# Two changes to a two-layer encoder kernel: keys and values turned in 32x32 blocks on VectorE, and the early gate and up weights split one part ahead

## The chip, the cores and the metric

The kernel runs on one core of one Trainium2 chip. A core has TensorE (matmuls and their weight loads), VectorE, ScalarE and GpSimd (POOL), and SyncE (SP), which here only issues DMAs; ScalarE and GpSimd issue some DMAs too. Matmul results land in PSUM (eight banks), all else is in SBUF (128 partitions) or in DRAM. The metric is the time of one execution on the device in microseconds; lower is better.

## The reference

What is computed, cut to what matters here (the convolution group, the gates and the norms are left out):

```python
for l in range(DEPTH):                                   # DEPTH = 2, D_MODEL = 1024
    h = h + hybrid_mixer(rmsnorm(h, norm1_w[l]), ...)    # 16 meta tokens + 1024 tokens = 1040 rows
    h = h + swiglu(rmsnorm(h, norm2_w[l]), w_gate_up[l], w_down[l])

# inside the mixer: 4 heads of 128, q and k normalised, v plain
qkv = jax.nn.silu(depthwise_conv_centred(qkv, conv_qkv_w))
o_fwd = chunk_gated_delta_rule(qp, kp, vp, gp[:, :, 0], bp[:, :, 0])
o_bwd = flip(chunk_gated_delta_rule(flip(qp), flip(kp), flip(vp), ...))

# the scan over chunks of tokens
v_new = u_c - w_c @ S
o     = qd_c @ S + a_c @ v_new
S     = S * gl_c + kd_c.T @ v_new

# swiglu
gate, up = jnp.split(h @ w_gate_up, 2, axis=-1)
return (jax.nn.silu(gate) * up) @ w_down
```

The products of the projections are made with each float32 operand split in two parts: a leading one (`hi`, cast on ScalarE) and the rest (`lo`, a subtraction on VectorE). A product is three matmuls: hi x hi, hi x lo, lo x hi.

## The kernel before, in words

**Layout.** Activations lie with channels on the 128 partitions and the 1040 tokens along the free dimension. A projection tile (`inproj`, L313, through `dense`, L144) makes 128 output channels for all tokens: 3 chunks of about 346 tokens (2 of 512 for some tiles of the second layer), each 8 x 3 matmuls into one PSUM bank (L156 to L158). Its weights come as two DMAs of 256 KB on SP (L125) into two `raw` buffers, are split by ScalarE (L126) and VectorE (L127) into three `whi`/`wlo` slots, and an evacuation on VectorE (L319 and others) multiplies by the row norm.

**Order of the work.** The kernel is written once, and a scheduler orders the instructions of each engine by priorities and a simulated time; after that every engine and every DMA queue runs its list in order. The program sets the priorities by hand: evacuations first (`evp`), dense matmuls late (`mmp`), and small jobs in between. Three lists (`jobs`, `jobs2`, `jobs3`) hold closures, and after each chunk of a dense tile one is taken from each list (end of `dense`).

**Stages of a layer.** First the key tiles and the query tiles (`seq`, L675), then four value tiles (L771), then the loop over `(4, 5, 0, 6, 7, 1, 2, 3)` (L805) with four `z` tiles and four convolution tiles (`sc_tile`, L781). Beside them run: `chunk_p` (L486), which makes key-by-key products for nine chunks of tokens (one of 16 meta tokens, eight of 128), `substitute` and `invert`, which invert the triangular matrices (VectorE, then small matmuls), and `chunk_a` (L520), query-by-key products. Then comes the scan (`scan_step`, L839): two directions, nine chunks, its matmuls laid among the dense ones of the convolution tiles and of half of the output projection (`w_out`), its tokens now on partitions. Then the other half of the output projection (`out_part`, L1035), the early gate/up parts, the gate/up tiles, the down projection.

**Turning keys and values.** The scan needs keys and values with tokens on the partitions. Before the change this is done with TensorE. `k_out` (L445), called by `chunk_p`, turns a chunk of keys: four transposes (L451) against an identity into PSUM bank "a", one copy by ScalarE (L453), one store on ScalarE's queue (L454) to `vkd[c, :, 1, :]` in DRAM. `v_store` (L749) does it for a value tile: one transpose of the 16 meta tokens (L753), a copy on VectorE (L757) and a store on SP (L760); and twice four transposes (L764), a copy by ScalarE (L765) and a store on its queue (L766) to `vkd[c, :, 0, :]`. The scan loads both with one row of 512 floats per token (L844, L846 on SP), ordered by head, then by channel. In the scan the keys are the stationary operand of the state update (`su`), the values are an operand of a VectorE addition (L879) and, in the first step, the moving operand.

Tiles of [128, 4, 128] come from one tag, `ck2`, of five buffers (`t2k`).

**The early parts.** While the last output tiles are made, the first products of the gate/up stage that do not need the second half of the tokens are done early: eight parts `(f, q)`, four gate/up rows by two halves of the input channels. `early_part` (L1139) loads 256 KB of weights (L1142), splits them (`w_op`, L1091 on ScalarE and L1092 on VectorE), and makes the product (`prod`, L1109, L1112, L1113), all in one call. Three parts are placed after output tiles 5, 6 and 7 (L1168), five behind the loop (L1199).

Of the kernel before, what the change touches and what calls it, by code (L numbers as in the profile page):

```python
# [17 lines left out]
L = 1040  # L18
H = 4
# [23 lines left out]
def trunk(ctx: ExitStack, tc: tile.TileContext, xT, w_in, w_ba, w_out, w_gu, w_dn,  # L43
# [27 lines left out]
    def pa():  # L71
        return bank("a")
# [229 lines left out]
    for l in range(DEPTH):  # L302
# [142 lines left out]
        def k_out(c, prev):  # L445

            n = 16 if c == 0 else 128
            s0 = 0 if c == 0 else 16 + 128 * (c - 1)
            ps = pa()
            for h in range(H):  # L450
                after(nc.tensor.transpose(ps[0:n, h * 128:(h + 1) * 128], KTt[:, h, s0:s0 + n], ident), prev if h == 0 else None)  # L451
            kt = t2k("kt")
            act(out=kt[0:n].rearrange("p a b -> p (a b)"), in_=ps[0:n], func=AF.Copy)  # L453
            adma(vkd[c, 0:n, 1, :], kt[0:n].rearrange("p a b -> p (a b)"))  # L454


        at0 = [sb.tile([16, 4, 16], F32, tag=f"at0{d}", name=nm("at0")) for d in range(2)]
        P0 = [sb.tile([16, 4, 16], F32, tag=f"P0{d}", name=nm("P0")) for d in range(2)]
# [27 lines left out]
        def chunk_p(c):  # L486
# [1 line left out]
            n, s0 = span(c)  # L488
            kk = bank("b").rearrange("p (h i) -> p h i", h=4)
            for h in range(H):  # L490
                end = mm(kk[0:n, h, 0:n], KTt[:, h, s0:s0 + n], KTt[:, h, s0:s0 + n], start=True, stop=True)
                if h == 0:
                    after(end, last_mm[0])
# [252 lines left out]
            mmp[0] = tc.cur_priority  # L746
            at_prio(here)

        def v_store(i, v, c0):  # L749

            ps = pa()
            if c0 == 0:
                low(lambda: nc.tensor.transpose(ps[0:16, 0:128], v[:, 0:16], ident))  # L753
                vm = t2k("vm")[0:16, 0, :]
                here = tc.cur_priority
                at_prio(evp[0])
                nc.vector.tensor_copy(vm, ps[0:16, 0:128])  # L757
                evp[0] = tc.cur_priority
                at_prio(here)
                dma(vkd[0, 0:16, 0, i * 128:(i + 1) * 128], vm)  # L760
            else:
                vt = v[:, 16 + 128 * (c0 - 1):16 + 128 * (c0 + 3)]
                for c in range(4):
                    low(lambda: nc.tensor.transpose(ps[:, c * 128:(c + 1) * 128], vt[:, 128 * c:128 * c + 128], ident))  # L764
                act(out=vt, in_=ps, func=AF.Copy)  # L765
                adma(vkd[c0:c0 + 4, :, 0, i * 128:(i + 1) * 128].rearrange("c p e -> p c e"), vt.rearrange("p (c e) -> p c e", c=4))  # L766

        ca = [0, 1, 8, 2, 7, 3, 6, 4, 5]
        st1 = sub_start(1)
        jobs3.extend([None, None, None, st1[0], st1[1], None, st1[2], st1[3], st1[4]])  # L770
        for i in range(4):  # L771
            t = trow()
            if i == 3:
                jobs3.extend([None] * 3 + invert(0))
            inproj(8 + i, to_row(t))
            v = trow() if i % 2 == 0 else row(Y[1] + "f")
            conv(t, v, P_CV + 3 * (8 + i))
            act(out=v, in_=v, func=AF.Silu)
# [60 lines left out]
        def scan_step(d, c, first, final, tied=False):  # L839
            n = 16 if c == 0 else 128  # L840
            s0 = 0 if c == 0 else 16 + 128 * (c - 1)
            base = d * 2048
            V, K, A, sz = (rec[:, base + 512 * i:base + 512 * i + 512].rearrange("p (h e) -> p h e", h=4) for i in range(4))
            dma(V[0:n].rearrange("p h e -> p (h e)"), vkd[c, 0:n, 0, :])  # L844
            if not final:
                dma(K[0:n].rearrange("p h e -> p (h e)"), vkd[c, 0:n, 1, :])  # L846
# [289 lines left out]
        early, bks0 = {}, {}  # L1136
        turn_e = [None]

        def early_part(f, q):  # L1139
# [22 lines left out]
        for m in range(KT + 2):  # L1162
# [514 lines left out]
```

## Time and profile before

| what | value |
|---|---|
| time, median of 3 runs | 2462.8 us |
| lowest and highest run | 2461.87 and 2466.39 us |
| the profiled execution, its own time | 2463.0 us |
| span of its instructions | 2461.2 us |
| TensorE busy | 2441.9 us (99%) |
| VectorE busy | 1782.3 us (72%) |
| ScalarE busy | 1056.0 us (43%) |
| DMA | 335.26 MB, mean 136 GB/s |

How to read it: times are in microseconds from the start of the span unless marked ns. PE is TensorE's matmul, PEld its weight load, DVE is VectorE, ACT ScalarE, SP SyncE; a "q" behind a name means that engine's sequencer or queue. L156 is line 156 of the kernel. A name such as `pacc<-a,whi` says which tile is written from which. A matmul's length in a row includes the time in the pipeline, so neighbours overlap; busy time counts a moment once. A row of busy times by stretch has the stretch, its length, then busy time and count for TensorE, its weight loads, VectorE, ScalarE and GpSimd, then the granted TensorE clock, the DMA share and GB/s.

### The profile page before, as it was taken

Reading aid. Unit: us, or ns where it says so; the run is one execution under the profiler, and the core shown is the slowest. Engines: PE = TensorE matmul, PEld = TensorE weight load, DVE = VectorE, ACT = ScalarE, POOL = GpSimd, SP = SyncE. Lnnn points to the kernel's source line nnn. Section 1 sums busy time; section 2 is a strip of 40 time slices with the busy share of each in tenths; the row PEclk is TensorE's granted clock in tenths of the full one; section 3 lists DMA queues with packets and bytes.
Section 4 is the critical chain, followed back from the end, with each engine's and each line's share of the span. In section 5 each row is a group of like instructions: output and inputs, shape, how many; then the busy total and the mean of one; then the engine's idle time right before and its main releaser. Section 6 shows DMA issues by size and latency. Waiting matters only on the chain. (4 is left out here: it accounts for less than half of the span.)

```text
span 2461.2 us, 44853 instructions
## 1 busy us (share of the span) xinstructions
PE 2441.9 (99%) x17530; PEld 2255.1 (92%) x17530; DVE 1782.3 (72%) x3296; ACT 1056.0 (43%) x1964; POOL 67.0 (3%) x157
## 2 busy tenths in 40 slices
PE   9999999999999999999999999999999999999998
PEld 8999999999999999999999988999978888888887
DVE  6888346769877777877657984457697777678774
ACT  6654434535333333444446543335453333234444
POOL 0120000000000000000000200000000000000002
PEclk9999999999999999999999999999999999999999
DMA  4445344534223332674224452445332233237641
GB/s 134 162 156 184 118 134 158 181 102 144 97 95 104 111 104 78 210 239 148 89 87 148 159 178 105 159 142 197 123 124 99 94 116 112 91 107 257 203 131 69
DMA packets 201320, 335.26 MB, mean 136 GB/s; under 512 B 23404, under 2 KB 88356, under 8 KB 201108
## 3 DMA queue, kind: packets, MB, share of 16 engines
q1 hardware_dynamic: 172996, 293.83, 36.0%
q10 hardware_dynamic: 25936, 34.19, 4.3%
q0 software_dynamic: 2176, 4.36, 0.6%
q8 instruction: 138, 2.26, 0.4%
q14 instruction: 74, 0.61, 0.1%
HBM read 250.31 MB, written 81.99 MB: 135 GB/s over the span
## 5 line engine op out<-in xcount | busy, mean ns | idle before, releaser
L156 PE MATMUL pacc<-a,whi 128*128 128x346 f32 (+1 forms) x800 | 260.2, 326 | 0.2 <-ACT a L176 0.2
L158 PE MATMUL pacc<-a,wlo 128*128 128x346 f32 (+1 forms) x800 | 259.0, 325 | 0.1
L156 PE MATMUL pacc<-b,whi 128*128 128x346 f32 (+2 forms) x672 | 232.4, 347 | 0.0
L158 PE MATMUL pacc<-b,wlo 128*128 128x346 f32 (+2 forms) x672 | 231.6, 346 | 0.3 <-DVE wlo L127 0.2
L157 PE MATMUL pacc<-a,whi 128*128 128x346 f32 (+1 forms) x681 | 221.9, 326 | 0.6 <-DVE a L177 0.6
L126 ACT ACTIVATE whi<-raw 128x512 fp32r<-128x512 f32 x166 | 104.6, 632 | 240.5 <-PE pacc L157 194.3
L157 PE MATMUL pacc<-b,whi 128*128 128x346 f32 (+2 forms) x580 | 200.1, 345 | 0.0
L156 PEld LDWEIGHTS pacc<-a,whi 128*128 128x128 f32 x800 | 150.5, 188 | 2.4 <-issue 1.0
L127 DVE TENSOR_TENSOR wlo<-raw,whi 128x512 fp32r<-128x512 f32 x166 | 114.2, 689 | 52.7 <-ACT whi L126 52.0
L158 PEld LDWEIGHTS pacc<-a,wlo 128*128 128x128 f32 x800 | 150.7, 189 | 1.4 <-issue 0.8
L158 PEld LDWEIGHTS pacc<-b,wlo 128*128 128x128 f32 x672 | 126.4, 188 | 10.5 <-issue 1.7
L156 PEld LDWEIGHTS pacc<-b,whi 128*128 128x128 f32 x672 | 126.4, 188 | 9.7 <-issue 0.8
L157 PEld LDWEIGHTS pacc<-a,whi 128*128 128x128 f32 x681 | 128.3, 188 | 4.7 <-issue 2.1
L1091 ACT ACTIVATE whi<-rw 128x512 fp32r<-128x512 f32 x92 | 57.9, 633 | 138.1 <-PE pf L1112 37.3
L157 PEld LDWEIGHTS pacc<-b,whi 128*128 128x128 f32 x580 | 109.2, 188 | 7.9 <-issue 1.0
L1091 ACT ACTIVATE b<-rw 128x512 fp32r<-128x512 f32 x64 | 40.2, 632 | 136.3 <-PE pacc L1112 38.9
L1091 ACT ACTIVATE a<-rw 128x512 fp32r<-128x512 f32 x64 | 40.2, 631 | 103.2 <-PE pacc L1112 62.6
L319 DVE TENSOR_TENSOR b<-pacc,rstd 128x346 f32<-128x346 f32 (+1 forms) x63 | 32.3, 513 | 48.8 <-PE pacc L158 48.7
L1092 DVE TENSOR_TENSOR wlo<-rw,whi 128x512 fp32r<-128x512 f32 x92 | 62.9, 686 | 2.9 <-ACT whi L1091 2.1
L319 DVE TENSOR_TENSOR a<-pacc,rstd 128x346 f32<-128x346 f32 (+2 forms) x59 | 32.7, 554 | 42.4 <-PE pacc L158 42.3
L1113 PE MATMUL pacc<-b,wlo 128*128 128x260 f32 (+1 forms) x172 | 52.7, 306 | 0.0
L1112 PE MATMUL pacc<-b,whi 128*128 128x260 f32 (+1 forms) x172 | 52.7, 306 | 0.0
(965 smaller groups left out, 7846.9 us busy)
## 6 DMA issues: line engine op xcount, KB each, us to landing
raw<-in_w_in SPq DMA_DIRECT2D x110, 256.0 KB
raw<-in_w_gu SPq DMA_DIRECT2D x104, 256.0 KB
rw<-in_w_gu SPq DMA_DIRECT2D x88, 256.0 KB
rw<-in_w_dn SPq DMA_DIRECT2D x94, 192.0 KB
rec<-vkd SPq DMA_DIRECT2D x61, 256.0 KB
raw<-in_w_out SPq DMA_DIRECT2D x48, 256.0 KB
b<-ad SPq DMA_DIRECT2D x45, 260.0 KB
a<-ad SPq DMA_DIRECT2D x45, 256.0 KB
```

What stands on the lines that cost most here:

```text
L126: whi_done[0] = act(out=hi, in_=raw[:, 0:kk, :], func=AF.Copy)
L127: whi_done[1] = tt(out=lo, in0=raw[:, 0:kk, :], in1=hi.bitcast(F32), op=ALU.subtract)
L156: mm(ps[:, :n], wh, xh[:, n0:n1], start=(i == 0), stop=False)
L157: mm(ps[:, :n], wh, xl[:, n0:n1], start=False, stop=False)
L158: last_mm[0] = mm(ps[:, :n], wl, xh[:, n0:n1], start=False, stop=(i == K - 1))
L319: tt(out=t[:, n0:n1], in0=ps, in1=rstd[:, n0:n1], op=ALU.mult)
L1091: act(out=hi, in_=src, func=AF.Copy)
L1092: tt(out=lo, in0=src, in1=hi.bitcast(F32), op=ALU.subtract)
L1112: mm(ps[:, :CW], w[0][:, k, :], tl[:, cs], start=False, stop=False, skip_group_check=True)
L1113: one = mm(ps[:, :CW], w[1][:, k, :], th[:, cs], start=False, stop=stop and k == nk - 1, skip_group_check=True)
```

## The change

`turned(c, w, src)` replaces the transposes on TensorE. VectorE transposes each 32x32 block of a [128, 4 heads, 128 tokens] tile, and writes it so that channel and head are interleaved, head fastest. A block transpose leaves a token's channels in four groups of 32 partitions, so four DMAs, one for each 32 channels, put them in place in `vkd`: runs of 128 floats (512 bytes). Two of the four of a key chunk go on ScalarE's queue, all others on SP. Values are first stored to DRAM as they are (`vd`, one store per tile on SP) and loaded back chunk by chunk for all four heads (`kv_load`), one job ahead of their transpose (`v_turn`). The nine keys and values are turned in ten jobs, put in the list when the fourth tile of the loop (the third `z` tile) begins; before, keys were turned in `chunk_p` and values right behind their tiles. In DRAM a token's row is now ordered by channel, then by head, so the scan's key and value operands have a step of four floats.

The early weights get a call of their own, `early_weights`, placed one part ahead of the product that uses them (two ahead in the last parts). The order of the parts is the same.

```diff
+        vd = dram.tile([4, 128, L], F32, name=nm("vd"))
+
+        def turned(c, w, src):
 
             n = 16 if c == 0 else 128
-            s0 = 0 if c == 0 else 16 + 128 * (c - 1)
-            ps = pa()
-            for h in range(H):
-                after(nc.tensor.transpose(ps[0:n, h * 128:(h + 1) * 128], KTt[:, h, s0:s0 + n], ident), prev if h == 0 else None)
-            kt = t2k("kt")
-            act(out=kt[0:n].rearrange("p a b -> p (a b)"), in_=ps[0:n], func=AF.Copy)
-            adma(vkd[c, 0:n, 1, :], kt[0:n].rearrange("p a b -> p (a b)"))
-
+            m = max(n, 32)
+            t = t2k("tn").rearrange("p a b -> p (a b)")[:, 0:4 * m].rearrange("p (j b h) -> p j b h", h=4, b=32)
+            nc.vector.transpose(out=t.rearrange("p j b h -> p h j b"), in_=src.rearrange("p h (j b) -> p h j b", b=32))
+            for i in range(4):
+                if c == 0:
+                    (adma if w and i > 1 else dma)(vkd[0, 0:16, w, 128 * i:128 * i + 128], t[32 * i:32 * i + 16, 0].rearrange("p b h -> p (b h)"))
+                else:
+                    (adma if w and i > 1 else dma)(vkd[c].rearrange("(j a) w e -> a j w e", a=32)[:, :, w, 128 * i:128 * i + 128], t[32 * i:32 * i + 32].rearrange("p j b h -> p j (b h)"))
+
+        def kv_load(c):
+
+            n, s0 = span(c)
+            m = max(n, 32)
+            t = t2k("vm")[:, :, 0:m]
+            dma(t, vd[:, :, s0:s0 + m].rearrange("h p t -> p h t"))
+            turned(c, 1, KTt[:, :, s0:s0 + m])
+            vload[c] = t
+
+        def v_turn(c):
+            turned(c, 0, vload.pop(c))
+
+        vload = {}
...
-            k_out(c, end)
...
-            jobs.extend([lambda i=i, v=v, c0=c0: v_store(i, v, c0) for c0 in (0, 1, 5)])
+            dma(vd[i], v)
...
             if j == 3:
                 jobs3.extend(invert(1))
+                jobs.extend([lambda i=i: (kv_load(ca[i]) if i < 9 else None, v_turn(ca[i - 1]) if i else None) for i in range(10)])
...
-            V, K, A, sz = (rec[:, base + 512 * i:base + 512 * i + 512].rearrange("p (h e) -> p h e", h=4) for i in range(4))
-            dma(V[0:n].rearrange("p h e -> p (h e)"), vkd[c, 0:n, 0, :])
+            V, K, A, sz = (rec[:, base + 512 * i:base + 512 * i + 512] for i in range(4))
+            dma(V[0:n], vkd[c, 0:n, 0, :])
             if not final:
-                dma(K[0:n].rearrange("p h e -> p (h e)"), vkd[c, 0:n, 1, :])
+                dma(K[0:n], vkd[c, 0:n, 1, :])
+            V, K = (t.rearrange("p (e h) -> p h e", h=4) for t in (V, K))
...
+        EARLY = [(0, 0), (1, 0), (0, 1), (1, 1), (2, 0), (3, 0), (2, 1), (3, 1)]
+        ew = {}
+
+        def early_weights(i):
+            f, q = EARLY[i]
             A = raw4("raw")
             dma(A, w_gu[l, f, 0, :, 4 * q:4 * q + 4, :])
-            w = w_op(A, True)
+            ew[f, q] = w_op(A, True)
+
+        def early_part(f, q):
+
+            w = ew.pop((f, q))
...
-            for f, q in {5: [(0, 0)], 6: [(1, 0)], 7: [(0, 1)]}.get(m, ()):
-                early_part(f, q)
+            if 5 <= m < 8:
+                early_part(*EARLY[m - 5])
+            if 4 <= m < 8:
+                early_weights(m - 4)
+            if m == 8:
+                early_weights(4)
...
-        for f, q in ((1, 1), (2, 0), (3, 0), (2, 1), (3, 1)):
-            early_part(f, q)
+        for i in range(3, 8):
+            early_part(*EARLY[i])
+            if 5 <= i + 2 < 8:
+                early_weights(i + 2)
```

The lines of `v_store` that go are told above.

More of the change, by code (lines that the diff above doesn't have):

```diff
@@ L443, in normalise @@
                 tt(out=dst[:, h, :], in0=dst[:, h, :], in1=bc, op=ALU.mult)
-        def k_out(c, prev):
+        vd = dram.tile([4, 128, L], F32, name=nm("vd"))
+        def turned(c, w, src):
             n = 16 if c == 0 else 128
-            s0 = 0 if c == 0 else 16 + 128 * (c - 1)
-            ps = pa()
-            for h in range(H):
-                after(nc.tensor.transpose(ps[0:n, h * 128:(h + 1) * 128], KTt[:, h, s0:s0 + n], ident), prev if h == 0 else None)
-            kt = t2k("kt")
-            act(out=kt[0:n].rearrange("p a b -> p (a b)"), in_=ps[0:n], func=AF.Copy)
-            adma(vkd[c, 0:n, 1, :], kt[0:n].rearrange("p a b -> p (a b)"))
+            m = max(n, 32)
[16 more added lines that the diff above has]
+        vload = {}
         at0 = [sb.tile([16, 4, 16], F32, tag=f"at0{d}", name=nm("at0")) for d in range(2)]
@@ L490, in chunk_p @@
             for h in range(H):
-                end = mm(kk[0:n, h, 0:n], KTt[:, h, s0:s0 + n], KTt[:, h, s0:s0 + n], start=True, stop=True)
+                one = mm(kk[0:n, h, 0:n], KTt[:, h, s0:s0 + n], KTt[:, h, s0:s0 + n], start=True, stop=True)
                 if h == 0:
-                    after(end, last_mm[0])
-            k_out(c, end)
+                    after(one, last_mm[0])
             for d in (dirs0 if c == 0 else (0, 1)):
@@ L747, in low @@
             at_prio(here)
[L749 to L766, printed above, removed]
         ca = [0, 1, 8, 2, 7, 3, 6, 4, 5]
@@ L842, in scan_step @@
             base = d * 2048
-            V, K, A, sz = (rec[:, base + 512 * i:base + 512 * i + 512].rearrange("p (h e) -> p h e", h=4) for i in range(4))
-            dma(V[0:n].rearrange("p h e -> p (h e)"), vkd[c, 0:n, 0, :])
+            V, K, A, sz = (rec[:, base + 512 * i:base + 512 * i + 512] for i in range(4))
+            dma(V[0:n], vkd[c, 0:n, 0, :])
             if not final:
-                dma(K[0:n].rearrange("p h e -> p (h e)"), vkd[c, 0:n, 1, :])
+                dma(K[0:n], vkd[c, 0:n, 1, :])
+            V, K = (t.rearrange("p (e h) -> p h e", h=4) for t in (V, K))
+            A, sz = (t.rearrange("p (h e) -> p h e", h=4) for t in (A, sz))
             if c > 0:
@@ L1137, in trunk @@
         turn_e = [None]
-        def early_part(f, q):
+        EARLY = [(0, 0), (1, 0), (0, 1), (1, 1), (2, 0), (3, 0), (2, 1), (3, 1)]
+        ew = {}
+        def early_weights(i):
+            f, q = EARLY[i]
             A = raw4("raw")
             dma(A, w_gu[l, f, 0, :, 4 * q:4 * q + 4, :])
-            w = w_op(A, True)
+            ew[f, q] = w_op(A, True)
+        def early_part(f, q):
+            w = ew.pop((f, q))
             if q == 0:
```

## The prediction

> **What bounds the kernel now.** I read the page first, then what TensorE waits for, then the busy time by stage.
>
> ```profile
> span 2461.2 us, 44853 instructions
> PE 2441.9 (99%) x17530; PEld 2255.1 (92%) x17530; DVE 1782.3 (72%) x3296; ACT 1056.0 (43%) x1964; POOL 67.0 (3%) x157
> PEclk9999999999999999999999999999999999999999
> ```
>
> TensorE is busy from end to end at the full granted clock, so what counts is what is taken from TensorE's own queue, and which waits it keeps. Its waits by releaser (total us, times, longest):
>
> ```profile
> PE pb L1113 <- DVE wlo L1092: 1.7, 2, 1.4
> PE pa L753 <- ACT b L765: 1.2, 1, 1.2
> ...
> PE pf L1113 <- DVE wlo L1092: 0.8, 1, 0.8
> ...
> PE pa L1113 <- DVE wlo L1092: 0.7, 1, 0.7
> ...
> PE pacc L158 <- DVE wlo L127: 0.2, 1, 0.2
> ```
>
> Two of these causes are touched: one value transpose that waited for its PSUM bank, and the early gate/up products (L1113) that waited for VectorE's half of the weight split. The stages, with TensorE, weight-load, VectorE and ScalarE busy time and counts:
>
> ```profile
> 150.00:215.00 65.00, 63.77 (x720) 60.56 (x719) 59.42 (x136) 34.20 (x46) 6.34 (x12) 1.00 0.38 120
> 260.00:310.00 50.00, 50.00 (x699) 47.62 (x698) 12.48 (x25) 19.14 (x35) 0.00 (x0) 1.00 0.34 116
> 563.00:605.00 42.00, 40.42 (x334) 39.23 (x333) 41.26 (x65) 26.45 (x48) 0.00 (x0) 1.00 0.39 126
> 1385.00:1455.00 70.00, 69.87 (x710) 62.06 (x709) 64.07 (x143) 34.91 (x46) 6.34 (x12) 1.00 0.43 137
> 1490.00:1550.00 60.00, 60.00 (x711) 52.52 (x710) 16.87 (x30) 20.90 (x38) 0.00 (x0) 1.00 0.34 117
> 1785.00:1830.00 45.00, 42.01 (x216) 33.31 (x215) 43.13 (x66) 26.49 (x42) 0.00 (x0) 1.00 0.41 135
> ```
>
> The rows are, for layers 0 and 1, the value rows (150, 1385), the stage to which the turning moves (260, 1490) and the early gate/up parts (563, 1785). VectorE is nearly full in the first kind, idle three quarters of the time in the second, and full in the third.
>
> **Part 1, what is removed.** A matmul's row shows its latency; what it costs is the distance to the next start. A block of four value transposes, then a single one (16 meta tokens), in the timeline of TensorE (start, length):
>
> ```profile
> 161.65 0.32 PE L158 MATMUL pacc<-a,wlo 128*128 128x346 f32 x1
> 161.81 0.60 PE L764 MATMUL pa<-ident,b 128*128 128x128 f32 x4
> 162.16 0.40 PE L156 MATMUL pacc<-a,whi 128*128 128x346 f32 x1
> 162.40 0.32 PE L157 MATMUL pacc<-a,whi 128*128 128x346 f32 x1
> ```
> ```profile
> 156.12 0.32 PE L157 MATMUL pacc<-a,whi 128*128 128x348 f32 x1
> 156.28 0.27 PE L753 MATMUL pa<-ident,b 128*16 128x128 f32 x1
> 156.31 0.41 PE L158 MATMUL pacc<-a,wlo 128*128 128x348 f32 x1
> 156.55 0.32 PE L156 MATMUL pacc<-a,whi 128*128 128x348 f32 x1
> ```
>
> From 161.65 to 162.40 are 0.75 us, in which two dense matmuls take 0.16 each (161.65 to 161.81 shows one): the block costs 0.75 - 0.32 = 0.43. The single one costs 0.43 - 0.32 = 0.11. Counts, from the whole span for L451 (keys), L764 and L753 (values); the two numbers after the stretch are busy time and count on TensorE, then on its weight loads:
>
> ```profile
> 0.00:2461.00 2461.00, 10.80 (x72) 8.41 (x72) 1.00 0.41 136
> 0.00:2461.00 2461.00, 9.76 (x64) 7.69 (x64) 1.00 0.41 136
> 0.00:2461.00 2461.00, 2.18 (x8) 0.70 (x8) 1.00 0.41 136
> ```
>
> 72 + 64 are 34 blocks: 34 x 0.43 = 14.6 us. Eight singles: 0.9 us. The bank wait of L753 goes too, since nothing else takes bank "a" there: 1.2 us. Together **-16.7 us**, all in TensorE's own queue. ScalarE's 34 copies out of PSUM and VectorE's eight go as well; they were beside TensorE's work, so I count nothing.
>
> **Part 1, what is added.** Per layer 18 block transposes on VectorE (16 of 512 columns, 2 of 128). The kernel has the same instruction on 1024 columns:
>
> ```profile
> L571 DVE STREAM_TRANSPOSE b<-x x1: 2192/2192/2192, 242.3 to 242.3; 128x1024 f32<-128x1024 f32 x1
> L571 DVE STREAM_TRANSPOSE a<-x x1: 2054/2054/2054, 1475.2 to 1475.2; 128x1024 f32<-128x1024 f32 x1
> ```
>
> About 1.05 us for half of it, so 16 x 1.05 + 2 x 0.3 = 17 us per layer. They lie in the stages that begin at 260 and 1490, where VectorE has 37.5 of 50 and 43.1 of 60 us free: hidden. Were the cover gone they would cost 34 us in all.
>
> DMAs: SP gains four stores of V rows, nine loads of turned-to-be values and 54 of the 72 quarter stores per layer, and loses four small stores; ScalarE gets the other 18 quarter stores and loses 17 stores. Issue costs:
>
> ```profile
> L846 SPq DMA_DIRECT2D rec<-vkd x31: 319/320/425, 295.8 to 1675.7; - x31
> L766 ACTq DMA_DIRECT2D vkd<-b x4: 366/369/378, 164.6 to 204.6; - x4
> ```
>
> POOL's queue is not passed. 63 x 0.37 = 23 us per layer on SP, which has no other work than to issue; on ScalarE one issue of 0.37 more, against 17 copies less. New waits: a value transpose waits on VectorE for its load, and behind it stand PSUM evictions (L319) and weight splits (L127); a quarter store waits on SP and on ScalarE for the transpose, and behind it stand the weight loads (L125), the scan's loads, and ScalarE's splits (L126). TensorE waits for the splits. Bounds: nothing (the value load is issued one job ahead of its transpose) up to rival B's sum. The nearest row, the wait for L127 above, is 0.2 us in the whole kernel; I take **+1 us**.
>
> The scan takes its loads from what the turning stores. It starts at 295 and 1534, and has slack: the last transposes of its output, and the first product that needs all of it:
>
> ```profile
> 499.90 0.60 PE L958 MATMUL pa<-ident,b3f 128*128 128x128 f32 x4
> ...
> 527.12 0.28 PE L156 MATMUL pf<-o,whi 128*128 128x260 f32 x1
> ...
> 1731.84 0.60 PE L958 MATMUL pa<-ident,a3f 128*128 128x128 f32 x4
> ...
> 1749.07 0.28 PE L156 MATMUL pf<-o,whi 128*128 128x256 f32 x1
> ```
>
> 27 and 17 us of dense matmuls follow it, so a scan that starts up to 17 us late costs nothing.
>
> The scan now reads keys and values with a step of four floats: 31 key tiles (the count of L846), four weight loads each, 124 in all, and the value operand of the VectorE additions. No row shows TensorE reading at such a step. Low end: nothing, and not below, as no work goes away. High end: the scan's matmuls start 0.112 us apart, eight of them in 0.90 us:
>
> ```profile
> 447.07 1.06 PE L861 MATMUL pb<-vv,P 128*128 128x128 f32 x8
> 447.97 1.06 PE L861 MATMUL pf<-vv,P 128*128 128x128 f32 x8
> ```
>
> A weight load twice as long adds 0.112 each: 124 x 0.112 = +13.9 us. The nearest row is VectorE's own: the transposes above, read or written at a step, take 2.0 to 2.1 ns a column, a plain operation less:
>
> ```profile
> L127 DVE TENSOR_TENSOR wlo<-raw,whi 128x512 fp32r<-128x512 f32 x166 | 114.2, 689 | 52.7 <-ACT whi L126 52.0
> ```
>
> That is 1.35 ns a column, a ratio of 1.5, but transposing itself may be the reason. On TensorE the load runs beside the matmul before it (92% and 99% busy on the page), so I take nothing and keep 13.9 as rival A. [...] On VectorE a slower value read would add some 0.13 us (128 columns at 1 ns) to each of four additions a step, 5 us in nine steps: inside the 17.
>
> **Part 2.** The early weights are loaded and split one part before they are used. At most the three L1113 rows go: 1.7 + 0.8 + 0.7 = 3.2 us. But VectorE is full in those stages (41.26 of 42, 43.13 of 45), the splits are only reordered, and TensorE then meets the next operand that VectorE owes. I take **-2 us** of 0 to -3.2.
>
> **Sum.** -16.7 + 1 - 2 = -17.7 us. The profiled execution took 2463.0 us (span 2461.2), 0.2 above the median of 2462.8; on the median that is **2445 us**.
>
> **The rivals.**
>
> A, strided keys: the reads above cost 13.9 us on TensorE, which has nothing to hide them: 2459. For it: the step is new, and the scan's TensorE work is dense. Against: the pairs are pipelined.
>
> B, slower than before: SP issues in order, and a quarter store that waits for a late value load holds the weight load behind it. Waits of SP between 260 and 310, and the longest landing in the chain that ended last:
>
> ```profile
> SPq L125 <- DVE wlo L127: 33.4, 5, 13.7
> ```
> ```profile
> 1819.71 6.11 DMA raw<-in_w_gu
> ```
>
> A load of 6.1, a transpose of 1.05 and four issues of 0.37 hold SP for 8.6 us. A weight slot comes free about one chunk (24 matmuls at 0.16 = 3.8 us) ahead of need, so TensorE would wait 4.8 us for each load caught. Five loads wait there per layer; from four caught in all (19 us) the gain is gone; at five to a layer, half of it overlapped with other waits, the sum is +24: 2469. For it: 63 more entries in that queue. Against: those five loads wait up to 13.7 us for their slot anyway, so the queue has time between them.
>
> C, VectorE becomes the bound in the crowded stages: the value rows' stage would shrink below its 59.4 and 64.1 us of VectorE work (I count 2 us lost per layer), and part 2 gives nothing back (2 us): 2451. For it: the busy rows above. Against: the last substitution steps on VectorE aren't needed until the next stage.
>
> **How the numbers follow.** Forecast 0.50, A 0.20, B 0.13, C 0.17. The bound for "same" is 0.2%, 4.9 us, about what a measurement of this kernel can tell from no change: 2457.9 to 2467.7. Faster: the forecast, C, and 0.07 of A (a partial penalty), 0.74. Same: 0.13 of A and 0.02 of B, 0.15. Slower: the rest of B, 0.11. The range reaches from all early stalls gone and some hidden transitions more (2438) to just past A (2461); outside lie B and a few hundredths of the others.
>
> **What would show it.** Right: no L451, L764 or L753 rows on TensorE, some 144 matmuls fewer, its busy time down by about 16 us; the 0.112 us spacing kept where the keys are weights; VectorE's new transposes near 1.05 us, in the stages with room; no new TensorE wait over 1 us. A: key products spaced 0.2 us. B: new TensorE waits for the splits between 260 and 310, behind SP waits for quarter stores. C: L1113 or L1109 waits as long as before. The forecast is wrong if the scan's end passes the first product that needs it, or if the key spacing grows.

## The result, and the profile after

| | before | after |
|---|---|---|
| time, median (lowest to highest) | 2463.9 us (2461.9 to 2466.4) | 2504.9 us (2502.4 to 2506.3) |
| ratio to before, 95% interval | 1 | 1.0165 [1.0147, 1.0182] |
| profiled execution, its span | 2463.0, 2461.2 us | 2506.3, 2504.3 us |

The forecast was 2445 us, and the range ended at 2461: wrong by 60 us, and in sign. The head of the page of after, span and busy time:

```profile
span 2504.3 us, 44778 instructions
PE 2475.6 (99%) x17386; PEld 2286.4 (91%) x17386; DVE 1823.3 (73%) x3324; ACT 1036.8 (41%) x1930; POOL 66.2 (3%) x157
```

TensorE has 144 matmuls fewer, and still it is busy 34 us longer. Two places show where. The first is the scan. The same group of matmuls at the same place of the work, in TensorE's timeline (start, length, count), before and then after:

```profile
452.63 1.05 PE L861 MATMUL pb<-vv,rec 128*128 128x128 f32 x8
453.51 0.61 PE L861 MATMUL pf<-vv,rec 128*128 128x128 f32 x4
453.96 1.06 PE L861 MATMUL pb<-vv,rec 128*128 128x128 f32 x8
454.85 1.50 PE L861 MATMUL pf<-vv,rec 128*128 128x128 f32 x12
456.11 0.40 PE L157 MATMUL pacc<-a,whi 128*128 128x346 f32 x1
```
```profile
470.53 1.05 PE L860 MATMUL pb<-vv,rec 128*128 128x128 f32 x8
471.42 1.09 PE L860 MATMUL pf<-vv,rec 128*128 128x128 f32 x4
472.35 2.03 PE L860 MATMUL pb<-vv,rec 128*128 128x128 f32 x8
474.21 1.99 PE L860 MATMUL pf<-vv,rec 128*128 128x128 f32 x12
475.96 0.40 PE L157 MATMUL pacc<-a,whi 128*128 128x346 f32 x1
```

Before, the 32 matmuls (16 float32 products of two each) take 3.48 us to the next dense matmul, after 5.43. Eight with attention tiles as weights (these lie in `rec` too) still take 0.89 us to the next start; the eight with keys as weights take 1.86 (472.35 to 474.21), 0.23 apart in place of 0.11. The weight loads (min/median/max ns) fit that:

```profile
L860 PEld LDWEIGHTS pf<-vv,rec x256: 186/256/332, 312.6 to 1775.2; 128*128 128x128 f32 x120, 16*128 16x128 f32 x8
L860 PEld LDWEIGHTS pb<-vv,rec x248: 187/193/332, 309.6 to 1748.5; 128*128 128x128 f32 x124
```

Together these are 504 loads for 252 products: 124 have keys as weights, 128 attention tiles. Before, all took 181 to 193 ns. Now 248, two for each product with keys, take more than 300, 330 in the median, and the other 256 at most 209.

The second place is the stage of the turning. A window of 60 us from 250 (PE busy and count, PEld, DVE, ACT, POOL, granted clock, DMA share, GB/s), before and then after:

```profile
250.00:310.00 60.00, 60.00 (x762) 57.62 (x761) 19.14 (x34) 22.73 (x40) 0.00 (x0) 1.00 0.36 123
```
```profile
250.00:310.00 60.00, 57.75 (x701) 54.14 (x700) 30.28 (x41) 20.71 (x37) 0.00 (x0) 0.91 0.70 199
```

TensorE gets through 61 matmuls fewer, waits 2.25 us and has 0.91 of its clock. The window after holds the same stage, though not quite the same instructions. VectorE has 30 us free in it, yet what counts is its order. VectorE's timeline, with the wait ahead of an instruction in brackets, and TensorE's:

```profile
269.37 1.06 DVE L452 STREAM_TRANSPOSE tn<-b 128x512 f32<-128x512 f32 x1
274.33 1.08 DVE L452 STREAM_TRANSPOSE tn<-vm 128x512 f32<-128x512 f32 x1 [3.90 <-DMA vkd<-tn]
275.26 0.67 DVE L127 TENSOR_TENSOR wlo<-raw,whi 128x512 fp32r<-128x512 f32 x1
```
```profile
273.41 0.33 PE L157 MATMUL pacc<-a,whi 128*128 128x348 f32 x1
275.98 0.43 PE L158 MATMUL pacc<-a,wlo 128*128 128x348 f32 x1 [2.25 <-DVE wlo L127]
```

A transpose needs one of the five `ck2` buffers, and waits 3.90 us until the quarter stores of an earlier chunk have landed and freed one. Behind it stands a weight split, and TensorE waits for that split. Then the clock drops. Six windows of after at half clock (the third column from the right):

```profile
277.20:284.00 6.80, 6.80 (x45) 6.31 (x44) 4.62 (x6) 3.78 (x7) 0.00 (x0) 0.50 0.93 259
304.50:307.90 3.40, 3.40 (x13) 3.40 (x13) 0.00 (x0) 1.10 (x4) 0.00 (x0) 0.51 0.86 255
314.80:318.20 3.40, 3.40 (x12) 3.40 (x13) 1.48 (x5) 0.00 (x0) 0.00 (x0) 0.50 0.58 211
1465.10:1471.90 6.80, 5.48 (x65) 5.41 (x65) 4.00 (x10) 1.76 (x3) 0.00 (x0) 0.50 0.48 170
1567.50:1574.30 6.80, 6.80 (x26) 6.03 (x24) 1.21 (x2) 2.27 (x7) 0.00 (x0) 0.50 0.70 239
1581.10:1584.50 3.40, 3.40 (x14) 3.40 (x13) 0.64 (x2) 0.00 (x0) 0.00 (x0) 0.50 0.32 111
```

30.6 us at half clock are about 15.3 us of work lost (an estimate from the clock of 0.50 in these rows; the account below has 15.7); before has such a window only at its very end. (After has a seventh, of 3.4 us at 55, ahead of all changed work; e4_early_only below, which turns on TensorE as before does, has it too.) TensorE's longest waits in after follow. The three of 2 us and more begin at 273.7, 1463.7 and 1562.4, close to the three long windows; the second window begins while its wait lasts.

```profile
PE pacc L158 <- DVE wlo L127: 3.7, 4, 2.2
PE pf L614 <- issue: 2.7, 1, 2.7
PE pb L860 <- DMA rec<-vkd: 2.0, 1, 2.0
```

**The account.** I gave each matmul the usual distance to the next start of its shape (lower quartile in before) and summed: that is TensorE's work. What the starts really took beyond it is the rest: slow loads, half clock and waits.

| kernel | span | matmuls | work | rest | of it waits and gaps over 1 us |
|---|---|---|---|---|---|
| before | 2461.2 | 17530 | 2350.6 | 102.5 | 5.2 |
| after | 2504.3 | 17386 | 2335.0 | 161.3 | 16.9 |
| e1_step_only | 2501.3 | 17530 | 2350.6 | 142.6 | 5.5 |
| e2_blocks | 2456.2 | 17386 | 2335.0 | 113.6 | 14.0 |
| e5_own_place | 2451.5 | 17386 | 2335.0 | 108.8 | 9.2 |
| e8_two_rings | 2453.2 | 17386 | 2335.0 | 110.6 | 13.5 |
| e9_in_place | 2457.4 | 17386 | 2335.0 | 114.8 | 13.4 |
| e13_two_behind | 2460.2 | 17386 | 2335.0 | 117.4 | 15.9 |

So 15.6 us of work went, and 58.8 us of rest came. Sorted by what a start met, of the 58.8 are 34.5 in scan matmuls with an operand from `rec` at full clock, 15.7 at half clock, 10.7 in waits of over 0.25 us, and -2.1 in everything else. The account is of one profiled execution for each kernel: that of e2_blocks was the fastest of its ten (5.2 us under their median), that of e8_two_rings also lies 5.2 under its median, that of e5_own_place 1.6 over it.

### The profile page after: what moved, and what is told of

Read it like the earlier page. It is cut to its first block, busy times and chain, and to the rows that moved or that the text cites. A ratio compares the mean times of both kernels' runs of the same rounds, so it can differ in the third digit from the quotient of the medians.

```text
span 2504.3 us, 44778 instructions
## 1 busy us (share of the span) xinstructions
PE 2475.6 (99%) x17386; PEld 2286.4 (91%) x17386; DVE 1823.3 (73%) x3324; ACT 1036.8 (41%) x1930; POOL 66.2 (3%) x157
## 5 line engine op out<-in xcount | busy, mean ns | idle before, releaser
L127 DVE TENSOR_TENSOR wlo<-raw,whi 128x512 fp32r<-128x512 f32 x166 | 113.9, 687 | 45.9 <-ACT whi L126 45.4
L1090 ACT ACTIVATE whi<-rw 128x512 fp32r<-128x512 f32 x92 | 57.8, 633 | 132.7 <-PE pf L1111 36.9
L1090 ACT ACTIVATE b<-rw 128x512 fp32r<-128x512 f32 x64 | 40.1, 630 | 141.1 <-PE pacc L1111 38.5
L1090 ACT ACTIVATE a<-rw 128x512 fp32r<-128x512 f32 x64 | 40.2, 630 | 103.7 <-PE pacc L1111 60.7
```

The lines of the kernel that those rows point to most:

```text
L127: whi_done[1] = tt(out=lo, in0=raw[:, 0:kk, :], in1=hi.bitcast(F32), op=ALU.subtract)
L1090: act(out=hi, in_=src, func=AF.Copy)
```

## The experiments

Theory S: the read at a step of four floats makes the loss. Rival theories: VectorE's or SP's queue in the turning stage, or part 2.

**e1_step_only**, before with the scan's views alone:

```diff
-V, K, A, sz = (rec[...].rearrange("p (h e) -> p h e", h=4) for i in range(4))
+V, K = (t.rearrange("p (e h) -> p h e", h=4) for t in (V, K))
+A, sz = (t.rearrange("p (h e) -> p h e", h=4) for t in (A, sz))
```

> The kernel before, in which only the scan's view of its key and value tiles is changed to a step of four floats; everything else, the TensorE transposes and the plain storage included, stays, so the channels and heads of keys and values reach the scan exchanged. Theory 1 (the step on TensorE): in the changed kernel the scan's pairs of weight load and matmul whose weights are keys stand 0.23 us apart instead of 0.112, and there are 248 of them, since each of the 124 float32 products is two pairs; so 248 x 0.12 = +30 us here: 2494 us, all of it in the scan. Theory 2 (waits): the changed kernel's loss comes from VectorE waiting for stores of turned tiles, the TensorE waits behind it and the half clock that follows; then this kernel, which has none of these, stays within 5 us of 2464.

Measured: 2503.5 us, ratio 1.0157 [1.0142, 1.0172]. The step alone costs 39 us, 9 more than theory 1 has; after is 41 us slower, with 15.6 us less work. The rest of e1 is 40.1 above before's, with 266 starts 0.215 to 0.26 us apart in the scan, where before has none. Its waits of over 1 us are before's (5.5 us against 5.2), and still it has two windows of 3.4 us at half clock in the scan (at 315 and 1574), where after has its windows at 314.8 and 1581.1.

**e2_blocks**, after with rows by block, head and channel, so that VectorE turns without a step on its output and the scan reads runs of 32 floats (the keys by four loads in place of one):

```diff
-t = ...rearrange("p (j b h) -> p j b h", h=4, b=32)
+t = ...rearrange("p (j h b) -> p j h b", h=4, b=32)
-dma(K[0:n], vkd[c, 0:n, 1, :])
+for i in range(4):
+    dma(K[0:n].rearrange("p (h i b) -> p i h b", h=4, i=4)[:, i], vkd[c, 0:n, 1, :].rearrange("p (i h b) -> p i h b", h=4, i=4)[:, i])
```

> The changed kernel with a token's row stored in blocks of 32 channels, head by head (block, head, channel) instead of channel by channel, so nothing has a step of four floats: the block transposes write runs of 32, keys are put in plain order by four loads of 128-byte runs in place of one, values are read in four runs of 32. Theory 1: the 248 key pairs go back to 0.112 us, -30 us, and the three half-clock windows inside the scan (10 us at half clock, 5 us) with them: 2470 to 2475 us. Theory 2: the waits stay as they are, 2500 to 2510 us. More DMA issues on SP (three more per key load, 93 in all) can cost a few us under both.

Measured: 2463.1 us, 0.9992 [0.9982, 1.0001], 7 us under the range of theory 1. All of the loss is gone, and of the 15.6 us of shorter work next to nothing is kept: 11.1 came back as rest in the profiled execution, and 14.3 by the medians (15.6 less the 1.3 us that it is faster than before). The transposes are faster too, by shape in after and then in e2_blocks:

```profile
L452 DVE STREAM_TRANSPOSE tn<-vm x18: 395/1089/1152, 253.3 to 1555.9; 128x512 f32<-128x512 f32 x16, 128x128 f32<-128x128 f32 x2
```
```profile
L452 DVE STREAM_TRANSPOSE tn<-vm x18: 302/711/715, 254.9 to 1528.8; 128x512 f32<-128x512 f32 x16, 128x128 f32<-128x128 f32 x2
```

Their length was not the price: VectorE still waits for buffers, 29.8 us against 26.4 in after (total, times, longest), and TensorE's wait for a split is still there:

```profile
DVE tn L452 <- DMA vkd<-tn: 29.8, 10, 7.3
```
```profile
PE pacc L158 <- DVE wlo L127: 2.7, 2, 2.4
PE pb L639 <- ACT P L646: 2.5, 1, 2.5
```

The second row, a wait in layer 1 at 1525, goes through ScalarE. Two of the four stores of a key chunk are on its queue; it issues four at 1519.39, 1519.89, 1522.71 and 1526.14, and the copies that TensorE needs come behind the last (the profile puts the end of that wait down to a value load):

```profile
1519.39 7.06 ACTq L457 DMA_DIRECT2D vkd<-tn  x4
1526.50 0.59 ACT L644 ACTIVATE a<-pb 64x512 f32<-64x512 f32 x1 [7.54 <-DMA vm<-vd]
```

**e3_turn_only** and **e4_early_only**: after without part 2, and before with part 2 alone.

```diff
 e3: -w = ew.pop((f, q))
 e3: +A = raw4("raw")
 e3: +dma(A, w_gu[l, f, 0, :, 4 * q:4 * q + 4, :])
 e3: +w = w_op(A, True)
 e4: the part-2 lines of the diff above, on before
```

> The changed kernel with the early parts as before (weights loaded and split in the same call as their product). If part 2 gives what was forecast, this is 2 us slower than the changed kernel: 2507. If the splits are only reordered and another operand is late instead, it is the same within 3 us: 2502 to 2508. If part 2 does harm, it is faster by 3 us or more.

> The kernel before with part 2 alone: 2462 us if the L1113 waits go as forecast (-2 of at most -3.2), 2464 if other operands are late in their place. Neither theory on the keys touches it.

Measured: e3 2503.9 us, 1.0155 [1.0138, 1.0171], and after 1.0165; e4 2464.6 us, 1.0000 [0.9991, 1.0010]. Part 2 is worth nothing that can be measured. TensorE's waits of after from 555 to 660 say why:

```profile
PE pacc L1108 <- DVE a L998: 1.3, 1, 1.3
PE pa L1112 <- DVE wlo L1091: 0.6, 1, 0.6
```

The splits come earlier, and the wait goes to the activations (L998) that the same VectorE owes; in layer 1 it goes to ScalarE's half of a split (L1090, 1.3 us).

Then the step itself, on before: **e6_values_step** has only the values at a step of four, **e7_keys_two** only the keys at a step of two.

```diff
 e6: +V = V.rearrange("p (e h) -> p h e", h=4)
 e7: +K = K.rearrange("p h e -> p (h e)").rearrange("p (g e k) -> p g k e", g=2, k=2)
```

> The kernel before with one change: only the values of a scan step are read at a step of four floats (channels and heads are exchanged in the values, so the output is another); the keys are read as before. e1_step_only, with both at the step, cost 39 us. Theory L (it is the weight load of the keys, 248 pairs at 0.23 us in place of 0.112): this costs only the first step's value products and at most 3 us of half clock, 2465 to 2470 us, and the scan's weight loads stay at 192 ns. Rival V (the values are read by VectorE between the first and the second group of products, 124 operations at 431 ns where before has 343, which would be 10.9 us if each stood on the path): 2475 us.

> The kernel before with one change: the keys of a scan step are read at a step of two floats, 8 bytes (heads and channels are exchanged in pairs, so the output is another); the values are read as before. It asks whether the price of the step is a threshold or grows with it. If the price grows with the bytes passed, a third of that at a step of four: a key pair spaced 0.15 us, 248 times 0.039, 2474 us. [...] If any step costs in full: 248 times 0.118 and half clock, 2495 us.

Measured: e6 2470.3 us, 1.0028 [1.0016, 1.0040]; e7 2465.5 us, 1.0005 [0.9995, 1.0014]. A step of two floats costs nothing that can be measured: neither 2474 nor 2495 us came, and the loads from `rec` take at most 201 ns. Four cost in full (up to 332 ns a load in e1_step_only), so the price does not grow evenly with the step; three was not tried, and why two are free and four are not is not shown. In e6 VectorE's operation with the values takes 430 ns in place of 343, 124 times (0.09 us each, 11 us in all), and the time leaves no room for that. What costs there is the first step, where the values are the moving operand (eight matmuls in 1.62 us to the next start, 0.80 in before):

```profile
303.18 1.98 PE L863 MATMUL pb<-rec,P 128*128 128x128 f32 x8
304.80 0.52 PE L158 MATMUL pacc<-a,wlo 128*128 128x346 f32 x1
```

30 starts in the scan are 0.215 to 0.26 us apart, 3.6 us, and two windows of 3.4 us at half clock follow (at 308 and 1550), 3.4 us. Measured are 5.6 us by the medians; the profiled execution, from which these sums are, was 2.6 over its median. So of e1's 39 us about 33 are the keys, by subtraction.

That left the turning. Theory W: VectorE stands in its order until a store has landed and freed a buffer, and what TensorE needs stands behind it. **e5_own_place** gives every turned tile but chunk 0's a place of its own:

```diff
-t = t2k("tn")...
+t = (KTt, QT)[w][:, :, s0:s0 + 128].rearrange("p j (h b) -> p j h b", b=32)
```

> The kernel with rows by block, head and channel (e2_blocks), and one change: except for chunk 0, the turned keys go into the chunk's slots of the query array and the turned values into its slots of the key array, which nobody reads any more at that point, in place of the ring of five 2-KB buffers. So a block transpose no longer waits until an earlier quarter store has landed and given a buffer back; operations, stores and loads are the same in number and size. In e2_blocks TensorE issues 15.6 us less work than before (2335.0 against 2350.6 us, each matmul at its usual spacing) but loses 11.1 us more in excess spacing (113.6 against 102.5), 8.8 of it in waits of over 1 us. Theory W (VectorE waits in order for buffers, the weight splits queued behind it come late, TensorE stops for over 2 us and then runs for some 3.4 to 7 us at half clock): the row of 29.8 us on turned buffers falls below 3 us, the wait of 2.4 us for a low weight part goes, and the time is 2449 to 2454 us. Rival S (the stores and value loads themselves are late, on SyncE or in the DMA): the wait comes back as a wait for a value load or for the records of the first scan step, and the time stays at 2459 to 2464.

The expectation is wrong in one thing: the scan still reads keys and queries from these arrays (its products with the state), so the output is another; operations and sizes are the same. Measured: 2451.6 us, 0.9949 [0.9934, 0.9964]. The wait for stores is gone from VectorE's list, from 230 to 310 the turned chunks wait 0.9 us for value loads (chunk 0's tile, still in the ring, 1.5 us for a buffer), and the window from 250 has its matmuls back. In layer 1 VectorE still waits 5.2 us for one value load, and TensorE does not wait for it.

```profile
DVE b L456 <- DMA vm<-vd: 0.9, 2, 0.5
```
```profile
250.00:310.00 60.00, 59.93 (x758) 57.24 (x757) 31.27 (x60) 25.24 (x41) 0.00 (x0) 1.00 0.67 189
```

11.5 us of e2_blocks come back. By stretch (110 to 235, 235 to 310, 1470 to 1590 us) the rest is 11.4, 5.6 and 6.7 in before, 15.6, 10.4 and 12.2 in e2_blocks, and 17.1, 6.2 and 6.4 in e5: in the two stages of the turning nothing of the loss is left. So the ring of five buffers is what costs there. Which way it costs is less sure, since the scheduler, once it had the places, also put the key transposes some 40 us earlier. The transposes of layer 0 in e2_blocks and then in e5 (keys from `b`, values from `vm`; first to last start):

```profile
L452 DVE STREAM_TRANSPOSE tn<-b x9: 311/702/711, 244.1 to 289.8; 128x512 f32<-128x512 f32 x8, 128x128 f32<-128x128 f32 x1
L452 DVE STREAM_TRANSPOSE tn<-vm x9: 302/711/715, 254.9 to 295.4; 128x512 f32<-128x512 f32 x8, 128x128 f32<-128x128 f32 x1
```
```profile
L456 DVE STREAM_TRANSPOSE b<-b x8: 700/702/707, 203.9 to 252.1; 128x512 f32<-128x512 f32 x8
L456 DVE STREAM_TRANSPOSE b<-vm x8: 669/700/711, 256.9 to 272.8; 128x512 f32<-128x512 f32 x8
```

So e5 has shorter waits and its transposes over a longer stretch, and no run parts the two.

Can a kernel with the right output have that? Six tries, on e2_blocks or on e9_in_place:

**e8_two_rings**: the turned values in the two halves of a row unused in that stage.

```diff
+t = t2k("tn")... if w else halves[ca.index(c) % 2]
```

> The kernel with rows by block, head and channel (e2_blocks), and one change: the turned values go into the two halves of a 4-KB row that lies unused in that stage, so that the ring of five 2-KB buffers serves only the value loads, the turned keys and the attention tiles: two buffers a chunk in place of three. Unlike in e5_own_place, which wrote over keys and queries that the scan still reads, nothing that is read later is overwritten. In e5_own_place, where no turned tile waits for a buffer, the time was 2451.6 us, 11.5 below e2_blocks. Theory W (the buffers that come free late are the price): most of that is kept, 2450 to 2455 us, and the wait for turned buffers is below 10 us in place of 29.8. Rival: two buffers for the values are as few as before, the wait stays near 30 us and the time at 2459 to 2464.

Measured: 2460.2 us, 0.9981 [0.9972, 0.9990]; the wait is still 24.9 us (12.8 and 12.1 for the two halves). The rival came true: two halves for all values are as few as before.

**e9_in_place**: values turned in the buffer in which they came, every second key tile in a half row. **e10_pool_queue**: two of four value stores on GpSimd's queue.

```diff
 e9: +nc.vector.transpose(out=src, in_=src)
 e10: -(adma if w and i > 1 else dma)(vkd[c]...
 e10: +(dma if i < 2 else adma if w else qdma)(vkd[c]...
```

> The kernel with rows by block, head and channel (e2_blocks), with fewer buffers needed a chunk: the values go to DRAM by block, head and column, come back as whole rows and are turned inside the buffer in which they came; of the turned keys every second goes into the two halves of a 4-KB row that lies unused in that stage. So a chunk takes one or two of the five buffers in place of three, and nothing that the scan reads is overwritten. In e8_two_rings (2460.2 us) the wait for turned buffers was still 24.9 us, because the two halves held the values of every chunk until SyncE had issued their four stores. Theory W (buffers that come free late, with the weight splits behind them): the wait falls below 8 us and the time comes to what e5_own_place had with a place for every tile, 2449 to 2455 us. Rival S (SyncE, which issues seven transfers a chunk at 0.43 us and more, is late by itself): the wait goes to the value loads or to the first records of the scan, and the time stays at 2458 to 2464.

> The kernel with rows by block, head and channel (e2_blocks), and one change: two of the four value stores of a chunk are issued by GpSimd in place of SyncE, so SyncE issues five transfers a chunk in place of seven; buffers are as in e2_blocks, three of five a chunk. Rival S (SyncE's issue holds the buffers): the wait for turned buffers falls to half of 29.8 us or less, and the time to 2450 to 2456 us. Theory W (three of five buffers a chunk are too few whoever issues, since a store takes 2.6 us from its issue to its landing): the wait stays over 20 us and the time at 2459 to 2465; GpSimd's own issue, 0.5 us and more for one in the kernel before, may make it later still.

Measured: e9 2461.1 us, 0.9987 [0.9978, 0.9996]; e10 2461.2 us, 0.9988 [0.9979, 0.9997]. In e10 the wait for stores is 25.1 us, so the two stores that SP no longer issues are not what holds the buffers. In e9 the wait for stores is 9.0 us in all (the longest row below has 5.6), but the value loads take its place, which is the sign of rival S:

```profile
DVE vm L462 <- DMA vm<-vd: 18.7, 8, 5.5
DVE vm L462 <- DMA vkd<-tn: 5.6, 2, 3.1
```

**e11_spread** and **e12_spread_in_place**: a chunk after every second group of columns, on e2 and on e9.

```diff
-jobs.extend([... for i in range(10)])
+for f in [... for i in range(10)]:
+    jobs.extend([f] + [None])
```

> The kernel with rows by block, head and channel (e2_blocks), and one change: a chunk is turned after every second group of columns of the projections in place of after every one, so nine chunks take twice the stretch; buffers, queues and sizes are as in e2_blocks. Shown so far: the turning takes 15.6 us off TensorE's work and puts 8 to 11 us of waits back; with a place for every turned tile (e5_own_place) 11.5 us of e2_blocks came back; with fewer buffers a chunk (e8_two_rings, e9_in_place) or with GpSimd's queue (e10_pool_queue) only 1 to 4, and the wait moved, in e9_in_place to value loads that had not landed (18.7 us). Theory P (pace: VectorE takes each transpose in its order, and at one chunk a group no chunk's loads and stores have landed when the next one wants them, whichever buffer or queue is made wider): with twice the time VectorE's waits for turned buffers and value loads fall from 34 us below 12, and the time to 2450 to 2455 us. Rival Q (the waits only move with the transposes, or the last chunks now come late for the scan): a wait for the scan's records or the same waits, 2459 to 2465 us.

> e9_in_place (values turned inside the buffer in which they came, every second key tile in the unused row) with the pace of e11_spread: a chunk after every second group of columns. Theory P: here neither a buffer nor a load is late, VectorE's waits for them are below 6 us in place of 24.3, and the time is 2449 to 2453 us, at or a little below e11_spread. Rival Q: as e9_in_place, 2459 to 2463 us. If e11_spread reaches 2450 to 2455 and this one no less, pace alone is the cause and buffers are no part of it; if this one is faster by 3 us or more, both are.

Measured: e11 2461.1 us, 0.9982 [0.9973, 0.9991]; e12 2458.7 us, 0.9971 [0.9959, 0.9982]. The waits are as long as without the change, 34.1 us for stores in e11 and 21.0 us for value loads in e12 (18.7 in e9). But this does not speak against theory P, for the edit did not change the pace. In e11 the transposes of layer 0 start as they do in e2_blocks, 2 to 3 us earlier throughout, and take as long from first to last:

```profile
DVE tn L452 <- DMA vkd<-tn: 34.1, 11, 7.8
L452 DVE STREAM_TRANSPOSE tn<-b x9: 311/702/712, 241.7 to 287.8; 128x512 f32<-128x512 f32 x8, 128x128 f32<-128x128 f32 x1
L452 DVE STREAM_TRANSPOSE tn<-vm x9: 298/711/712, 252.5 to 293.1; 128x512 f32<-128x512 f32 x8, 128x128 f32<-128x128 f32 x1
```

In e12 the values are turned from 244.9 to 285.7, in e9 from 245.7 to 284.9. The calls stand further apart in the program and the instructions do not; the scheduler places those by priorities and a simulated time. So theory P was not tested. (The sentence in the expectation of e13 below that the pace isn't the cause rests on this run, and falls with it.)

**e13_two_behind**: e9 with the values turned two groups after their load.

```diff
-v_turn(ca[i - 1]) if i else None) for i in range(10)
+v_turn(ca[i - 2]) if i >= 2 else None) for i in range(11)
```

> e9_in_place (values turned inside the buffer in which they came, every second key tile in the unused row), and one change: the values of a chunk are turned two groups of columns after their load is issued, in place of one. In e9_in_place VectorE still waited 18.7 us for value loads to land, in 8 places, and 5.6 us for stores; e11_spread, at half the pace, kept its 34.1 us, so the pace isn't the cause. Theory W (VectorE takes a transpose in its order and stands there until a transfer has landed, be it the store that frees its buffer or the load that fills it, and the weight splits behind it stand too): with the load a group earlier the wait falls below 10 us and the time to 2450 to 2456 us. Rival Q (three loads in flight need buffers that are still held, so the wait returns as one for stores or as a late load): over 15 us of waits and 2457 to 2463 us.

Measured: 2461.4 us, 0.9985 [0.9976, 0.9994]. The time is the rival's, and the wait is one for value loads. Here too the edit did not do what was meant: from the issue of a value load to the start of its transpose are 4.2 us in the median, as in e9, so no load got a longer lead. Whether a longer one would help stays open.

```profile
DVE vm L462 <- DMA vm<-vd: 21.8, 11, 4.2
```

The lowest median among the versions that compute the reference is that of e12_spread_in_place, 0.3% below before, 1.8% below after, and 7 us above e5_own_place; its interval overlaps with those of the other five tries. How to keep those 7 us with the right output stays open.

## Why the prediction was wrong, point by point

- **The transposes' 16.7 us: right but for 1.2.** The account has 15.6 us less work, against 15.5 for the blocks and singles. The 1.2 us for the bank wait of L753 did not show: it stood in before at 203.4, and after waits 1.25 us at 208.9, at a product of the inversion (L613).
- **The step, "so I take nothing and keep 13.9 as rival A": this is the step that failed.** The prediction put it at nothing; e1_step_only measured 39 us. The mechanism of rival A was the right one, and its size was too small as well. First, 124 loads was a wrong count. In these traces a float32 product is two pairs of load and matmul (504 loads for 252 products; the group of eight in 0.90 us that the prediction shows is four products), so keys are loaded 248 times, and the spacing grew by 0.12 (0.112 to 0.23): 30 us. Second, the first steps' value products (3.6 us in e6) and half clock add most of the rest of the 39. That a load "runs beside the matmul before it" did not cover the longer one: the load grew by 0.138 us (192 to 330 ns), and the spacing of the pairs by nearly as much (0.12). The nearest row, VectorE's ratio of 1.5, spoke for a price and I set it aside.
- **"a scan that starts up to 17 us late costs nothing": no cover for TensorE.** The scan's products lie among dense matmuls in one queue. A slower product is TensorE's own time, and so is a late one: in layer 1 of after SP issues 13 quarter stores in the 7.2 us ahead of the scan's first load, and TensorE stands 2.0 us for it (the third row of its waits above). For VectorE's reads "inside the 17" held: 0.09 us each (343 to 430 ns in e6), where 0.13 was estimated at 1 ns a column (in before, 512 columns take 689 ns at L127 and 1024 take 1220 at L1454, 1.04 for each further column).
- **New waits, "+1 us": failed, it is 11.1** (the rest of e2_blocks above before's; 14.3 by the medians). I compared VectorE's free time (37.5 of 50 us) with the transposes' length, and their 1.09 us came as estimated. But it isn't length that costs: in e2_blocks a transpose takes 0.71 us and the waits stay (29.8 us). A transpose that waits for a buffer (3.90 us in after) holds the splits behind it (TensorE waits 2.25 us there), and a store that waits on ScalarE holds its copies (TensorE waits 2.5 us in e2_blocks). I named those queues and priced them by a row of a kernel that has no such wait. e5_own_place shows the five buffers to be the cause of most of it, 11.5 us; whether by the waits or because the keys are then turned earlier is not shown.
- **Part 2, -2 us: nothing** (e3, e4). The sentence that TensorE then meets the next operand that VectorE owes was right in layer 0, and should have been the term; in layer 1 it is one that ScalarE owes.
- **Rival B** had the side right and the mechanism mostly wrong: TensorE did wait for splits between 260 and 310, but behind VectorE, not behind SP's weight loads. Only the 2.0 us of the scan's first load lie on SP's queue. **Rival C** came true in part: part 2 gives nothing back. In the crowded stretch from 110 to 235 the rest is 0.5 above before's in after, but 4.2 in e2_blocks, 5.7 in e5 and 6.1 in e12, with waits of about 2 us at 126 to 128 for VectorE (L513, line numbers of after) and 6.8 to 10.2 us at half clock. No run tried what makes it come and go.
- What the parts leave: e1 (+40.1 of rest) and e2 (+11.1) make 51.2 of the 58.8. By the medians, where e2 is not at its fastest, only 3 us are left over. Of the 7.6 in the profiles 2.4 lie at half clock and 3.3 in waits; what makes these longer with both parts is not shown (the transposes take 1.09 us there against 0.71).

## What to carry to other kernels

Before a layout puts a step into an operand of TensorE, count the weight loads by their rows (here a float32 product has two: 248 for the 124 with keys) and price each as exposed: here the loads of back-to-back small products set the pace (192 to 330 ns a load, 0.112 to 0.23 us a pair). When work moves to an engine with free time, ask for each instruction what it can wait for there (a buffer, a store, a load) and what stands behind it; free time covers length, not waits (VectorE had 30 of 60 us free in after, and TensorE waited 2.25 us behind one of its transposes). Waits of 2.0 to 2.7 us on TensorE lay close to the three windows of 6.8 us at half clock in after: such a wait may cost twice, once as a wait and once as clock, but that it is the cause was not tried. And read an edit back in the trace: where a scheduler places the instructions, calls that were moved (e11 to e13) need not move them, and a buffer that was added (e5) can.

## What the runs showed that I had not expected

- A step of four floats: 192 to 330 ns a load, 0.112 to 0.23 us a pair; a step of two: at most 201 ns a load, 1.0005 of the time (e7).
- VectorE's block transpose of 128x512 takes 1.09 us when it writes at a step of four floats, 0.71 without (e2).
- Half clock came in windows of 3.4 to 10.2 us, apart from the one at the end of each kernel. Waits of 2.0 to 2.7 us stood ahead of the long ones in after, one of 1.25 us ahead of the window at 211 in e2_blocks, and none of over 0.3 us but a burst of slow reads ahead of that at 308 in e6; waits of 1.2 and 1.4 us in before had none behind them. That the waits are the cause was not tried by itself.
- With the calls of the turning at double the distance (e11) every transpose stayed within about 3 us of its place in e2_blocks.
